# Eight long products, then eight short ones: the order of matmuls within a projection's chunk

## Chip, cores and metric

The kernel runs on one core of one Trainium2 chip. The metric is the device time of one execution in microseconds, from the start of the program to its end.

## What is computed

Two layers of an encoder on 256 tokens with 1024 channels, in float32. Cut to what matters here:

```python
def layer(h):
    xn = rmsnorm(h, norm1)                       # 256 x 1024
    u, q, k, v, g_pool, g_attn = split(xn @ w_in)  # 1024 -> 1024 + 3*1536 + 2*1024
    pool_out = (windowed_means(u) - u) @ w_pool * pool_scale
    attn_out = dilated_attention(q, k, v, rel_bias)       # 12 heads in 3 groups
    merged = sigmoid(g_pool) * (pool_out @ w_a) + sigmoid(g_attn) * (attn_out @ w_b)
    h = h + merged @ w_o
    a, g = split(rmsnorm(h, norm2) @ w_up)       # 1024 -> 2 * 2816
    return h + (gelu(conv3(a)) * g) @ w_down     # 2816 -> 1024
```

A last rmsnorm follows the second layer. The weights are some 162 MB in all and are read once.

## The kernel before

All large products use a faster float32 format of TensorE that keeps fewer bits (`F32R`). To keep the accuracy, each operand is written as a high part and a rest, `a = ah + al` and `w = wh + wl`, and a product is made of three: `wh*ah + wh*al + wl*ah`.

The class `Weights` brings the weights. SyncE loads pieces of 1 MB into one of three `raw` buffers. ScalarE casts half of such a piece into `wh` (L177), and VectorE subtracts to make `wl` (L178). There are five buffers each of `wh` and `wl`, and the splits run some three pieces ahead of TensorE. A buffer is free again when the last matmul that reads it has run.

A *chunk* is 128 output channels of a projection, for all 256 tokens. `proj` takes the next piece, of shape 128 x 8 x 128 (`KD` = 8 steps of 128 input channels), and calls `two_sums`. The normalised input lies in `x2`, channels on partitions, as [128, 8, part, 256 tokens], so that the high parts and the rests of one step stand side by side as 512 columns. `two_sums` makes, for each of the eight steps, one matmul with `wh` on all 512 columns (L482), which writes `wh*ah` into the left half and `wh*al` into the right half of one PSUM tile, and one matmul with `wl` on the 256 columns of high parts (L483), which adds `wl*ah` to the right half. All 16 add up in the same tile, `proj_ps`. Then ScalarE copies the right half out (L503) and VectorE adds the left (L504), or like steps in the attention's query and key code. There are four such PSUM tiles.

`proj` is called 192 times: for the pooled branch's input, the queries and keys, the projection with `w_a` (input `po`), both gates and both halves of `w_up`. The product with `w_b` (`b_ps`, input `at`) calls `two_sums` too, 16 times, with four steps instead of eight. Other products do not go through it: the values (L578, L653, L740) and the residual products with `w_o` and `w_down` (L508 to L510) have runs of 512 columns, and the pooled product (L474 to L476) and the attention have 256 columns or 128.

The attention's work is cut into steps (`scores`, `turn`, `weigh`) which are called between chunks. `turn` transposes the probabilities on TensorE (L903), eight of 128 columns for a head.

Each engine runs its own queue in order. A scheduler of the tile framework sets the order within each queue as the program is built, by an estimate of when operands will be there; on TensorE it may put other matmuls between those of one chunk.

Of the kernel before, what the change touches and what calls it, by code (L numbers as in the profile page):

```python
# [204 lines left out]
def encoder(ctx, tc, x, w_in, w_pool, pool_scale, w_a, w_b, w_o, norm1, norm2, w_up, conv_w,  # L205
# [272 lines left out]
    def two_sums(ps, wh, wl, x2, nk):  # L478


        for k in range(nk):
            nc.tensor.matmul(ps, wh(k), x2[:, k], start=(k == 0), stop=False)  # L482
            nc.tensor.matmul(ps[:, 1], wl(k), x2[:, k, 0], start=False, stop=(k == nk - 1))  # L483

    def proj(x2):

        i, (wh, wl) = W.get()
        ps = mmp.tile([P, 2, S], F32, tag="mm", name="proj_ps")
        two_sums(ps, lambda k: wh[:, k, :], lambda k: wl[:, k, :], x2, KD)
        W.free(i)  # L490
        return ps[:, 0], ps[:, 1]
# [256 lines left out]
    for l in range(DEPTH):  # L748
# [251 lines left out]
        for c4 in range(2):  # L1000
            ths = [gate(4 * c4 + j) for j in range(4)]
            for j2 in range(2):
                i, (wh, wl) = W.get()
                for j in range(2):
                    c = 4 * c4 + 2 * j2 + j
                    ps = mmp.tile([P, 2, S], F32, tag="mm", name="b_ps")
                    cc = slice(j * P, (j + 1) * P)
                    two_sums(ps, lambda k: wh[:, k, cc], lambda k: wl[:, k, cc], at2, 4)
                    m = sm.tile([P, S], F32, tag="u", name="m")
                    add_up(m, (ps[:, 0], ps[:, 1]))  # L1010
                    nc.vector.scalar_tensor_tensor(
                        out=m, in0=ths[2 * j2 + j], scalar=1.0, in1=m, op0=ALU.add, op1=ALU.mult
                    )
                    nc.vector.tensor_add(out=m, in0=m, in1=pa[:, c, :])
                    m = halves(m)
                    nc.scalar.copy(out=mh[:, c], in_=m)
                    nc.vector.tensor_sub(out=ml[:, c], in0=m, in1=mh[:, c].bitcast(F32))
                W.free(i)
# [152 lines left out]
```

## Time and profile before

| | us |
|---|---|
| median of 3 runs | 885.79 (885.66 to 886.0) |
| the profiled execution | 885.33 |
| its span | 883.5 |
| TensorE busy (PE) | 875.9, 99% of the span |
| weight loads (PEld) | 755.9, 86% |
| VectorE busy (DVE) | 676.8, 77% |
| ScalarE busy (ACT) | 520.2, 59% |
| DMA | 164.47 MB, 186 GB/s |
| granted clock of TensorE | 0.998 |

PE is TensorE's matmuls, and PEld its weight loads, which run beside them. A row of a group names the line, the engine and operation, the tiles (out<-in), the shapes and the count, then the busy time and the mean duration in ns, then the idle time before it. The line numbers are those of the kernel before. Starts in the timeline are in us from the start of the span; in the trace they are whole nanoseconds, and where single steps are given in ns they are differences of two such starts. Matmuls are pipelined and overlap, so that the step from one start to the next is shorter than the duration.

Where the stages lie, in us of the span: first values until 41, pooled input 41 to 79, queries, keys, attention and the projection with `w_a` 79 to 178, gates and `w_b` 179 to 234, `w_o` 234 to 257, the MLP 257 to 442; the second layer in the same order from 442 on, with its MLP from 691 to 877.

### The profile page before, as it was taken

What the parts mean: (1) busy time and instruction counts of PE and PEld (TensorE: products, weight loads), DVE (VectorE), ACT (ScalarE), POOL (GpSimd) and SP (SyncE); (2) the same over time, 40 slices, a digit from 0 to 9 for tenths busy, and PEclk for the clock granted to TensorE, in tenths of its full rate; (3) what the DMA queues carried; (4) which work ended last, traced back from release to release, by engine and by line L of the source; (5) the groups of instructions that cost most, each with busy time, mean ns of one, the idle gap of its engine ahead of it and who ended that gap; (6) DMA issues with size and microseconds to landing.
All of it is one profiled execution on the core that took longest, in us unless ns stands there. A gap on an engine that the chain in (4) does not pass through costs nothing.

```text
span 883.5 us, 12773 instructions
## 1 busy us (share of the span) xinstructions
PE 875.9 (99%) x4849; PEld 755.9 (86%) x4849; DVE 676.8 (77%) x1151; ACT 520.2 (59%) x913; POOL 13.1 (1%) x40
## 2 busy tenths in 40 slices
PE   9999999999999999999999999999999999999997
PEld 7889889888888888888888898889888888888886
DVE  6988785767869977877855977766778698787784
ACT  7745554556647756666645564554566477666663
POOL 1000000000000000000000000000000000000000
PEclk9999999999999999999999999999999999999999
DMA  9669744455555475465736555444556447455541
GB/s 332 230 205 307 239 145 144 143 179 188 185 187 191 146 236 190 154 227 191 239 119 213 168 191 191 143 152 134 191 191 218 156 154 231 172 198 187 187 144 48
DMA packets 125790, 164.47 MB, mean 186 GB/s; under 512 B 2995, under 2 KB 106107, under 8 KB 125600
## 3 DMA queue, kind: packets, MB, share of 16 engines
q1 hardware_dynamic: 125712, 163.65, 55.7%
q8 instruction: 38, 0.62, 0.3%
q14 instruction: 24, 0.20, 0.1%
q10 hardware_dynamic: 16, 0.00, 0.0%
HBM read 162.57 MB, written 3.69 MB: 188 GB/s over the span
## 4 chain that ended last, share of the span: by engine, by line
PE 99%; ACT 0%; POOL 0%; DVE 0%; issue 0%; POOLq 0%; ACTq 0%
PE proj_ps L482 41%; PE proj_ps L483 20%; PE res_ps L508 6%; PE res_ps L510 6%; PE v_ps L578 6%; PE res_ps L509 6%; PE v_ps L740 2%; PE b_ps L482 2%; PE v_ps L653 1%; PE pt_ps L903 1%; PE b_ps L483 1%; PE o_ps L924 1%; PE s_ps L874 1%; PE s_ps L869 1%; PE o_ps L920 1%; PE xt_ps L450 1%
## 5 line engine op out<-in xcount | busy, mean ns | idle before, releaser
L482 PE MATMUL proj_ps<-x,wh 128*128 128x512 f32 x1408 | 498.5, 398 | 0.0
L178 DVE TENSOR_TENSOR wl<-raw,wh 128x1024 fp32r<-128x1024 f32 x274 | 334.4, 1223 | 123.5 <-ACT wh L177 121.3
L177 ACT CAST wh<-raw 128x1024 fp32r<-128x1024 f32 x274 | 286.6, 1051 | 189.4 <-PE proj_ps L482 146.2
L483 PE MATMUL proj_ps<-x,wl 128*128 128x256 f32 x1408 | 394.1, 280 | 0.0
L482 PEld LDWEIGHTS proj_ps<-x,wh 128*128 128x128 f32 x1408 | 264.5, 188 | 63.6 <-issue 0.7
L483 PEld LDWEIGHTS proj_ps<-x,wl 128*128 128x128 f32 x1408 | 265.6, 189 | 0.9 <-issue 0.2
L508 PE MATMUL res_ps<-wh,actq 128*128 128x512 f32 (+1 forms) x184 | 70.5, 383 | 0.0
L510 PE MATMUL res_ps<-wh,actk 128*128 128x512 f32 (+1 forms) x184 | 70.1, 381 | 0.0
L509 PE MATMUL res_ps<-wl,actq 128*128 128x512 f32 (+1 forms) x184 | 70.0, 380 | 0.0
L482 PE MATMUL proj_ps<-po,wh 128*128 128x512 f32 x128 | 46.2, 402 | 0.0
L510 PEld LDWEIGHTS res_ps<-wh,actk 128*128 128x128 f32 x184 | 34.6, 188 | 7.0
L508 PEld LDWEIGHTS res_ps<-wh,actq 128*128 128x128 f32 x184 | 34.6, 188 | 6.9
L509 PEld LDWEIGHTS res_ps<-wl,actq 128*128 128x128 f32 x184 | 34.6, 188 | 6.2
L483 PE MATMUL proj_ps<-po,wl 128*128 128x256 f32 x128 | 35.7, 279 | 0.0
L1084 ACT ACTIVATE y<-a,prm 128x256 f32<-128x256 f32 x36 | 21.6, 599 | 18.9 <-DVE a L504 18.8
L1101 ACT ACTIVATE y<-y 128x256 f32<-128x256 f32 x44 | 18.3, 416 | 21.3 <-DVE y L1098 21.3
L482 PEld LDWEIGHTS proj_ps<-po,wh 128*128 128x128 f32 x128 | 24.0, 188 | 5.0
L416 ACT ACTIVATE junk<-h 128x512 f32<-128x512 f32 (+1 forms) x20 | 10.9, 547 | 27.7 <-DVE h L414 27.7
L508 PE MATMUL res_ps<-wh,m 128*128 128x512 f32 (+1 forms) x72 | 26.5, 368 | 0.0
L510 PE MATMUL res_ps<-wh,m 128*128 128x512 f32 (+1 forms) x72 | 26.3, 366 | 0.0
L509 PE MATMUL res_ps<-wl,m 128*128 128x512 f32 (+1 forms) x72 | 26.3, 365 | 0.0
L578 PE MATMUL v_ps<-wh,x 128*128 128x512 f32 x80 | 25.7, 392 | 0.0
(208 smaller groups left out, 1129.6 us busy)
## 6 DMA issues: line engine op xcount, KB each, us to landing
raw<-in_w_in_dram SPq DMA_DIRECT2D x58, 1024.0 KB, 5.4
raw<-in_w_up_dram SPq DMA_DIRECT2D x44, 1024.0 KB, 5.1
raw<-in_w_down_dram SPq DMA_DIRECT2D x22, 1024.0 KB, 4.9
raw<-in_w_a_dram SPq DMA_DIRECT2D x8, 1024.0 KB, 4.9
raw<-in_w_o_dram SPq DMA_DIRECT2D x8, 1024.0 KB, 4.9
raw<-in_w_b_dram SPq DMA_DIRECT2D x4, 1024.0 KB
sk<-fd SPq DMA_DIRECT2D x1, 2560.0 KB
raw<-in_w_pool_dram SPq DMA_DIRECT2D x2, 1024.0 KB
```

What stands on the lines that cost most here:

```text
L177: lambda: nc.scalar.copy(out=h, in_=src),
L178: lambda: nc.vector.tensor_sub(out=l, in0=src, in1=h.bitcast(F32)),
L416: nc.scalar.activation(junk[:, 0 : cc.stop - cc.start], h[:, t, cc], AF.Square, scale=D**-0.5, accum_out=ss[:, n : n + 1],)
L482: nc.tensor.matmul(ps, wh(k), x2[:, k], start=(k == 0), stop=False)
L483: nc.tensor.matmul(ps[:, 1], wl(k), x2[:, k, 0], start=False, stop=(k == nk - 1))
L508: nc.tensor.matmul(ps, ah, wh, start=first, stop=False)
L509: nc.tensor.matmul(ps, ah, wl, start=False, stop=False)
L510: nc.tensor.matmul(ps, al, wh, start=False, stop=last)
L578: nc.tensor.matmul(ps, x2[:, 2 * n + j, part, t, :], w[:, j, :], start=(n + m == 0), stop=(n == 3 and m == 5),)
L740: nc.tensor.matmul(ps[t], a[:, k, t, :], w[:, j, :], start=(k + m == 0), stop=(k == KD - 1 and m == 2),)
L1084: nc.scalar.activation(y, a, AF.Identity, bias=b, scale=w1)
L1101: nc.scalar.activation(y2, y2, AF.Tanh, scale=c)
```

## The change

In `two_sums` the loop over the steps is split into two. The eight products with `wh` on 512 columns come first, and then the eight with `wl` on 256 columns. In `b_ps` it is four and four. What is added up is the same; the order of the additions in the right half of the tile differs.

```diff
     def two_sums(ps, wh, wl, x2, nk):
 
 
         for k in range(nk):
             nc.tensor.matmul(ps, wh(k), x2[:, k], start=(k == 0), stop=False)
+        for k in range(nk):
             nc.tensor.matmul(ps[:, 1], wl(k), x2[:, k, 0], start=False, stop=(k == nk - 1))
```

## Prediction

> **What bounds the kernel now.** I read the page's totals first, then the chain, the groups and the waits.
>
> ```profile
> span 883.5 us, 12773 instructions
> PE 875.9 (99%) x4849; PEld 755.9 (86%) x4849; DVE 676.8 (77%) x1151; ACT 520.2 (59%) x913; POOL 13.1 (1%) x40
> PE 99%; ACT 0%; POOL 0%; DVE 0%; issue 0%; POOLq 0%; ACTq 0%
> L482 PE MATMUL proj_ps<-x,wh 128*128 128x512 f32 x1408 | 498.5, 398 | 0.0
> L177 ACT CAST wh<-raw 128x1024 fp32r<-128x1024 f32 x274 | 286.6, 1051 | 189.4 <-PE proj_ps L482 146.2
> L483 PE MATMUL proj_ps<-x,wl 128*128 128x256 f32 x1408 | 394.1, 280 | 0.0
> ```
>
> TensorE is the bound from the first microsecond to the last six. Idle time before the two product groups is 0.0. All its waits together are two:
>
> ```profile
> PE gain_ps L333 <- DVE ones L319: 1.0, 1, 1.0
> PE v_ps L653 <- ACT xuh L609: 0.2, 1, 0.2
> ```
>
> So time can only come from, or go to, the spacing of matmuls. The durations of the groups (398 and 280 ns) do not give it, since matmuls overlap; the step from one start to the next in the timeline does. In two stretches where nothing but pairs of a 512 and a 256 column product runs, with the clock at full speed in both:
>
> ```profile
> 181.58 0.39 PE L482 MATMUL proj_ps<-x,wh 128*128 128x512 f32 x1
> ...
> 209.31 0.39 PE L482 MATMUL proj_ps<-x,wh 128*128 128x512 f32 x1
> ```
>
> ```profile
> 286.80 0.40 PE L482 MATMUL proj_ps<-x,wh 128*128 128x512 f32 x1
> ...
> 300.93 0.40 PE L482 MATMUL proj_ps<-x,wh 128*128 128x512 f32 x1
> ```
>
> The first holds 10 chunks of 8 pairs: 27.73 us / 80 = 346.6 ns a pair. The second holds 5 chunks: 14.13 us / 40 = 353.3 ns. The instructions are the same; the layout of the start times is not. In the tight rhythm the steps are 231 and 112 ns, then 233 and 117, and so on; in the loose one 233 and 117, 241 and 120, 236 and 113, repeated. A pair costs 6.7 ns more there.
>
> What would runs of one width cost? The down projection (L508 to L510) gives runs of 512 columns, the pooled product (L474 to L476) a run of 256:
>
> ```profile
> 387.67 0.40 PE L508 MATMUL res_ps<-wh,actq 128*128 128x512 f32 x1
> ...
> 390.00 0.39 PE L509 MATMUL res_ps<-wl,actq 128*128 128x512 f32 x1
> ...
> 391.36 0.39 PE L509 MATMUL res_ps<-wl,actq 128*128 128x512 f32 x1
> ```
>
> ```profile
> 512.10 0.28 PE L475 MATMUL pool_ps<-pll,wh 128*128 128x256 f32 x1
> ...
> 513.06 0.40 PE L482 MATMUL proj_ps<-x,wh 128*128 128x512 f32 x1
> 513.29 0.28 PE L483 MATMUL proj_ps<-x,wl 128*128 128x256 f32 x1
> ```
>
> From 390.00 on, six steps take 1.36 us: 226.7 ns each, and it stays there. But the first ten, right behind the pairs, take 2.33 us: 233.1 each (241, 237, 234, 236, 224, 231, 236, 228, 233, 231). A run of 512 therefore begins with a settling time of up to 64 ns. The run of 256 is at 0.96 us / 8 = 120.0 ns, and the 512 behind it takes 233. 226.7 + 120.0 = 346.7 is exactly the tight pair. I call that the base, and all above it the excess.
>
> **The change, part by part.** Nothing is added or removed: 4849 matmuls and loads before and after, each with its own load. In the built program the chunks stand on TensorE in the same order, except that one chunk in each layer's attention, which was cut in two by transposes, is now whole.
>
> *Excess now.* I took every step of the 1597 pairs, less 226.7 or 120.0. 43 steps are more than 40 ns over (the first product behind 128 column transposes, 313 ns instead of 227, and the bias products); they are 3.6 us and stay. The rest is 6.46 us: 0.55 in 79 to 112 us, 1.99 in 269 to 441, 1.16 in 479 to 545, 1.99 in 703 to 876, 0.78 in the attention and early stretches, and nothing in 59 to 79, 179 to 234 and 612 to 668, which are in the tight rhythm. This is all that a new order can win.
>
> *Excess after.* A chunk becomes eight steps of 512 behind a run of 256, then eight of 256 behind a run of 512. The second join is in the trace at 874 us and twice more: 113, 119, then 120 throughout, 8 ns below the base. The first step of the first join is too: 233 ns, 7 over. How a run of 512 goes on from there is not, since the trace has only a 256 next. Bounds: from above, the ten steps at 387.67, whose first eight are 54 ns over; from below, the entry at 303.76, 236 and then at once 227, 9 ns over. Between them lies the entry of 234.27 (231, 224, 231, 236, 228, 232, 231, then 227), 27 ns over. I line the unknown run up with places where a 512 starts in the same phase. Settled starts keep one place on a grid of 6.67 ns (the tight pair is 52 such units, the loose one 53), and the start behind the 233 lies up to a nanosecond short of the settled place; in the trace, starts there go on 236, 228, 232, 231, 227 more often than straight to 227. So I take 7 + 20 = 27 over, less the 8 of the short run: 20 ns a chunk, three units, between 0 and 46.
>
> - 192 chunks of `proj` x 20 ns = 3.84 us.
> - 16 half chunks of `b_ps`, now at the base: 7 + 9 + 2 + 5 in four steps, less 8: 15 ns, +0.24 us.
> - 16 runs of the down projection now follow a run of 256 and not pairs: 14 settle in 27 instead of 64 ns, two in 27 instead of 9: -0.48 us.
> - The two whole chunks save one return from transposes each, 86 ns: -0.2 us with what goes with it.
> - Removed: 6.46 us.
>
> The sum is 3.84 + 0.24 - 0.48 - 0.2 - 6.46 = -3.06 us. Against the profiled execution's 885.33 (883.5 of span and 1.8 around it) that is 882.3; the median of the runs is 0.46 higher, so 882.7.
>
> [...]
>
> *Costed at nothing.* ScalarE splits a weight (L177) when its `wh` buffer is free, which comes 7 x 120 = 0.84 us earlier; 146.2 us of its idle time wait for that, but TensorE never waited for the splits, so this is only more lead; the loads on SyncE follow the split and keep their order. `wl` is needed 7 x 227 = 1.6 us later than before, so VectorE's L178 gets lead too. The last product of a chunk is still a 256 into the second half, so the reads (L503, L504) start as before. VectorE's and ScalarE's own orders shift around the attention. The one tight place:
>
> ```profile
> 119.73 0.48 DVE L891 TENSOR_SCALAR p<-p,rz 128x512 f32<-128x512 f32 x1
> 120.28 0.64 PE L903 MATMUL pt_ps<-ident,p 128*128 128x128 f32 x4
> ```
>
> The second four transposes start 0.07 us behind their input. They now stand right behind the first four, 0.7 us earlier, and the cut chunk no longer covers them. In the new order of VectorE the scaling L891 stands one weight split (1.22 us) earlier, which covers it. Without that cover it costs 0.7 us a layer, 1.4 in all, everything behind it on TensorE included.
>
> **The rivals.**
>
> *No settling time.* Behind the 233 the run goes straight to 227, as at 303.76. Each chunk is then at the base: -6.46 - 0.8 (down projection) - 0.2 = -7.5, 878.3 us. For it: the start lies less than a nanosecond from the settled place. Against: most starts there go on unsettled.
>
> *Every chunk settles anew, at length.* As at 387.67: each of the eight steps of 512 pays about a unit, and the short run behind it undoes the settling, so that the next chunk pays again. 192 x (54 - 8) = 8.83, b_ps 16 x (41 - 8) = 0.53, less 6.46 and 0.2: +2.7, 888.5 us. For it: 14 of 16 entries behind pairs go this way, and the eight steps end before the ten of settling do. Against: those entries start with 241, not 233. It decides from 34 ns a chunk on (6.46 us / 192), five units. The stretches that are now in the tight rhythm would lose, 2.77 to 2.82 us a chunk.
>
> *Order is free.* The excess has a cause outside the order (who starts when, which rhythm a stretch fell into), and the mean of tight and loose stays: 885.8, or a few tenths beside it. Four or five units a chunk give much the same. [...] For it: three stretches of pairs are at the base already. Against: the rhythm changes where the widths change, behind runs.
>
> **How the numbers follow.** Forecast 0.42, no settling 0.14, order free or near the break-even 0.17, settling at length 0.27. The likeliest gives 882.7; its own range is two to four units, 881.4 to 884.0 at 1.28 us a unit (192 x 6.67 ns). The range that leaves out 2 in 10 takes in both outer cases: 878.2 to 888.6. About 0.2% (1.8 us) is what a measurement of this kernel can tell from no change. Faster: 0.14 and most of 0.42, 0.52. Same: 0.17 and the slow edge of the forecast, 0.20. Slower: 0.28.
>
> **What would show it.** Step by step: chunks at 2.79 us from start to start everywhere, in the stretches of 179 to 234 us (2.773 now) as in 269 to 441 (2.826 now); inside a chunk 233, 236, 228, 232, 231, 227, 227, 227 and 113, 119, 120. The first stretch should get slower by 0.3 us and the second faster by 1.2. Chunks all at 2.773 show the first rival, at 2.82 the second, unlike chunks in unlike stretches the third. An idle TensorE before L903 or L482 would be the lost cover. I am wrong if the step behind a long run of 256 is not 226.7 to 241 ns at all, for example if eight short products in a row outrun their weight loads and go above 120.

## The result, and the profile after

| | before | changed |
|---|---|---|
| median of 6 runs, us | 885.71 (885.02 to 886.0) | 881.88 (881.74 to 882.35) |
| the profiled execution, us | 885.33 | 882.29 |
| its span, us | 883.5 | 880.5 |

The ratio of the medians is 0.996, with a 95% interval of 0.995 to 0.997. The changed kernel is faster by 3.8 us by the medians and by 3.0 us between the two profiled executions. The forecast was 882.7 us, and 882.3 for a profiled execution.

The page of the changed kernel, its totals, chain and groups:

```profile
span 880.5 us, 12819 instructions
PE 872.5 (99%) x4849; PEld 759.1 (86%) x4849; DVE 676.9 (77%) x1151; ACT 520.3 (59%) x913; POOL 13.8 (2%) x40
PE 99%; ACT 0%; POOL 0%; DVE 0%; issue 0%; POOLq 0%; ACTq 0%
...
L482 PE MATMUL proj_ps<-x,wh 128*128 128x512 f32 x1408 | 354.1, 393 | 0.0
...
L484 PE MATMUL proj_ps<-x,wl 128*128 128x256 f32 x1408 | 196.3, 282 | 0.0
```

TensorE still carries 99% of the chain, and the two product groups still have no idle time before them. What looks like a large change is none: the busy time of L482 fell from 498.5 to 354.1 us and that of the short products from 394.1 to 196.3 us, though the mean of one instruction hardly moved (398 to 393 ns, 280 to 282 ns). Overlapping records of one line are now neighbours, and busy time counts an overlap once. All of PE fell by only 3.4 us, which is the real gain.

The waits of TensorE are the same two:

```profile
PE gain_ps L333 <- DVE ones L319: 1.0, 1, 1.0
PE v_ps L654 <- ACT xuh L610: 0.2, 1, 0.2
```

So the time came out of the spacing of matmuls. The timeline of TensorE in the two stretches that the prediction showed (start, time, instruction):

```profile
181.54 2.00 PE L482 MATMUL proj_ps<-x,wh 128*128 128x512 f32 x8
...
209.47 0.86 PE L482 MATMUL proj_ps<-x,wh 128*128 128x512 f32 x3
```

```profile
284.21 2.00 PE L482 MATMUL proj_ps<-x,wh 128*128 128x512 f32 x8
286.05 1.12 PE L484 MATMUL proj_ps<-x,wl 128*128 128x256 f32 x8
...
300.97 0.86 PE L482 MATMUL proj_ps<-x,wh 128*128 128x512 f32 x3
```

From 181.54 to 209.47 are ten chunks in 27.93 us, 2.793 each (2.773 before): this stretch became slower. From 284.21 to 300.97 are six chunks in 16.76 us, also 2.793 each (2.826 before). Unlike stretches have become alike. Inside a chunk the eight long products take 1.84 us and the eight short ones 0.95. By single starts the steps are 233, 236, 228, 233, 231, 226, 227, 227 and then 113, 119, 120 six times: 20 ns above the base. Of the 191 chunks whose products stand in one piece, 143 take 2793 or 2794 ns from their first start to the next product's.

Eighteen chunks are cheaper. Seventeen stand behind a run of 512, as this one behind the values (L579); the other is the kernel's first, with only two small transposes between:

```profile
269.82 1.98 PE L482 MATMUL proj_ps<-x,wh 128*128 128x512 f32 x8
271.63 1.12 PE L484 MATMUL proj_ps<-x,wl 128*128 128x256 f32 x8
272.59 0.60 PE L1059 MATMUL a_turn<-ident,a_rows 128*128 128x128 f32 x4
```

From 269.82 to 272.59 is 2.77 us: the width does not change at the chunk's start, all eight long steps are 226 or 227, and the short run begins with 113 as everywhere.

### The profile page after: what moved, and what is told of

Its sections match the earlier page's. It is cut to its first block, busy times and chain, and to the rows that moved or that the text cites. A ratio compares the mean times of both kernels' runs of the same rounds, so it can differ in the third digit from the quotient of the medians.

```text
span 880.5 us, 12819 instructions
## 1 busy us (share of the span) xinstructions
PE 872.5 (99%) x4849; PEld 759.1 (86%) x4849; DVE 676.9 (77%) x1151; ACT 520.3 (59%) x913; POOL 13.8 (2%) x40
## 4 chain that ended last, share of the span: by engine, by line
PE 99%; ACT 0%; POOL 0%; DVE 0%; issue 0%; POOLq 0%; ACTq 0%
PE proj_ps L482 40%; PE proj_ps L484 21%; PE res_ps L510 6%; PE res_ps L509 6%; PE v_ps L579 6%; PE res_ps L511 6%; PE v_ps L741 2%; PE b_ps L482 2%; PE v_ps L654 1%; PE b_ps L484 1%; PE s_ps L875 1%; PE o_ps L925 1%; PE pt_ps L904 1%; PE s_ps L870 1%; PE o_ps L921 1%; PE xt_ps L450 1%
## 5 line engine op out<-in xcount | busy, mean ns | idle before, releaser
L482 PE MATMUL proj_ps<-x,wh 128*128 128x512 f32 x1408 | 354.1, 393 | 0.0
L482 PEld LDWEIGHTS proj_ps<-x,wh 128*128 128x128 f32 x1408 | 254.1, 189 | 47.4 <-issue 0.5
L484 PEld LDWEIGHTS proj_ps<-x,wl 128*128 128x128 f32 x1408 | 192.0, 190 | 13.8
L484 PE MATMUL proj_ps<-x,wl 128*128 128x256 f32 x1408 | 196.3, 282 | 0.0
L482 PE MATMUL proj_ps<-po,wh 128*128 128x512 f32 x128 | 33.1, 400 | 0.0
L482 PEld LDWEIGHTS proj_ps<-po,wh 128*128 128x128 f32 x128 | 22.9, 189 | 4.1
L579 PE MATMUL v_ps<-wh,x 128*128 128x512 f32 x80 | 25.7, 392 | 0.0
L1086 DVE SCALAR_TENSOR_TENSOR y<-a,prm,y 128x255 f32<-128x255 f32 x36 | 17.2, 479 | 8.1 <-ACT y L1085 8.1
```

The lines of the kernel that those rows point to most:

```text
L579: nc.tensor.matmul(ps, x2[:, 2 * n + j, part, t, :], w[:, j, :], start=(n + m == 0), stop=(n == 3 and m == 5),)
L1086: nc.vector.scalar_tensor_tensor(out=y[:, 1:], in0=a[:, : S - 1], scalar=w0, in1=y[:, 1:], op0=ALU.mult, op1=ALU.add)
```

## Experiments

The theory is the prediction's: a change of width costs TensorE a *settling* of some steps, short ones give some of it back, and what a chunk costs above the base depends on how its widths are laid out. The rivals are three: the gain is the lead that the splits of the weights got (`wl` needed later, `wh` free earlier); the excess belongs to alternating two weights rather than two widths; or it belongs to stretches and not to the order.

For each kernel I added up the excess of all steps behind products of `proj` (a start to the next, less 226.7 or 120.0; steps over 40 ns left out, as in the prediction). It is 6.42 us before and 3.34 in the changed kernel. (The prediction has 6.46 for the first; a base of 226.67 ns in place of 226.7 makes about that difference.) The *stream* is the time from the first product of the first chunk to the start of the last matmul, in the profiled execution of each kernel. It leaves out the start of the program, which no order here touches and which took 41.6 to 42.4 us in these executions. The kernel before, run again beside each, gave medians of 885.2 to 885.6 us.

| kernel | us, median | stream, us | proj excess, us | chunk in the MLP behind short products, ns above its base |
|---|---|---|---|---|
| before: runs of 1 | 885.7 | 835.0 | 6.42 | 37 to 58 |
| runs of 2 | 880.15 | 829.9 | 2.29 | 13 |
| runs of 4 | 884.64 | 833.8 | 5.24 | 33 |
| changed: runs of 8 | 881.88 | 831.3 | 3.34 | 20 |
| one long first | 884.17 | 833.1 | 3.93 | 20 |
| two chunks: runs of 16 | 881.79 | 831.2 | 1.53 | 10 |
| two chunks outside | 880.59 | 830.0 | 2.08 | 10 |
| steered | 879.79 | 829.2 | 0.85 | 0 in most, 5 to 8 in others |

**The lead or the layout.** One long product, then the eight short ones, then the other seven long. The runs have the changed kernel's lengths, read cyclically, but `wl` is needed as early as before.

```diff
-        for k in range(nk):
-            nc.tensor.matmul(ps, wh(k), x2[:, k], start=(k == 0), stop=False)
+        nc.tensor.matmul(ps, wh(0), x2[:, 0], start=True, stop=False)
         for k in range(nk):
-            nc.tensor.matmul(ps[:, 1], wl(k), x2[:, k, 0], start=False, stop=(k == nk - 1))
+            nc.tensor.matmul(ps[:, 1], wl(k), x2[:, k, 0], start=False, stop=False)
+        for k in range(1, nk):
+            nc.tensor.matmul(ps, wh(k), x2[:, k], start=False, stop=(k == nk - 1))
```

> Each chunk is one 512, eight 256, seven 512. Across chunks that is again one run of eight 512 (seven of one chunk, one of the next) and one run of eight 256, as in the changed kernel, but wl is needed after one product instead of eight and wh comes free at the end. Settling theory (the cost is paid once per join of a short run to a long one, whatever the place of the join in the chunk): again 2.793 us from chunk to chunk, total within 0.5 us of the changed kernel, 881.4 to 882.4 us. Lead theory (the gain came from wh coming free early and wl being wanted late): the gain goes back, 885 to 886 us, with idle time of TensorE before the first 256 of a chunk.

Measured: 884.17 us (883.82 to 885.36), 0.9989 of before, 0.998 to 0.9998. The total lies between the ranges of both theories, so neither had it; the spacing decides. In the timeline of this kernel:

```profile
276.17 0.39 PE L481 MATMUL proj_ps<-x,wh 128*128 128x512 f32 x1
276.39 1.11 PE L483 MATMUL proj_ps<-x,wl 128*128 128x256 f32 x8
...
298.51 0.39 PE L481 MATMUL proj_ps<-x,wh 128*128 128x512 f32 x1
```

Eight chunks from 276.17 to 298.51 are 22.34 us, 2.793 each, the changed kernel's chunk without its lead, and the waits view has no wait ahead of a short product. So the lead is not the gain. But the stream of matmuls is 1.8 us longer than the changed kernel's, elsewhere. The largest piece, 0.74 us, is a wait of transposes at the end of the first layer's MLP. In the waits view and in VectorE's timeline:

```profile
PE xt_ps L450 <- DVE xn L441: 0.5, 1, 0.5
```

```profile
440.46 0.48 DVE L441 SCALAR_TENSOR_TENSOR xn<-h,rstd,gain 128x256 f32<-128x256 f32 x1 [1.85 <-POOL rstd L428]
440.87 0.68 DVE L414 TENSOR_TENSOR h<-res_ps,h 128x512 f32<-128x512 f32 x1
441.47 1.27 DVE L441 SCALAR_TENSOR_TENSOR xn<-h,rstd,gain 128x256 f32<-128x256 f32 x3
```

The scheduler put the sum L414 in front of three of the four normalisations; in the changed kernel three normalisations come first:

```profile
439.14 1.28 DVE L441 SCALAR_TENSOR_TENSOR xn<-h,rstd,gain 128x256 f32<-128x256 f32 x3 [1.84 <-POOL rstd L428]
440.34 0.68 DVE L414 TENSOR_TENSOR h<-res_ps,h 128x512 f32<-128x512 f32 x1
```

Another 0.57 us are the transposes of the probabilities, which wait behind VectorE too, and 0.59 the proj steps. These places are read from the profile; no kernel tested them by themselves. An order in `two_sums` also reorders VectorE; the two waits here are 1.3 us, a third of the 3.7 us by which the changed kernel's stream is shorter than that of before.

**Shorter runs.** In groups of four and four; the kernel of twos has 2 for each 4 of the new lines:

```diff
-        for k in range(nk):
-            nc.tensor.matmul(ps, wh(k), x2[:, k], start=(k == 0), stop=False)
-        for k in range(nk):
-            nc.tensor.matmul(ps[:, 1], wl(k), x2[:, k, 0], start=False, stop=(k == nk - 1))
+        for k0 in range(0, nk, 4):
+            for k in range(k0, k0 + 4):
+                nc.tensor.matmul(ps, wh(k), x2[:, k], start=(k == 0), stop=False)
+            for k in range(k0, k0 + 4):
+                nc.tensor.matmul(ps[:, 1], wl(k), x2[:, k, 0], start=False, stop=(k == nk - 1))
```

> Four 512, four 256, four 512, four 256 in a chunk: twice the joins. Settling theory: the 4 + 4 products of b_ps in the changed kernel cost 16.6 ns over the base, so a chunk costs 2 x 16.6 = 33 ns over it instead of 20: 2.806 us a chunk, 192 x 13 ns = 2.5 us more than the changed kernel, 884.4 us. Order-is-free theory: no difference to the changed kernel, 881.9, or the old time, 885.7.

> Two 512 and two 256 in turn: four joins a chunk. Settling theory: the first two steps of a settling run are 7 and 9 ns over, and the two of the short run some 4 to 8 under: 8 to 12 ns a join, 32 to 48 a chunk against 20 now and some 34 on the average in turn: 2.805 to 2.821 us a chunk, 884.2 to 887.3 us. Order-is-free theory: 881.9 or 885.7, with different chunks in different stretches.

Fours: 884.64 us (884.26 to 885.44), as expected. A chunk has the steps 233, 236, 228, 233 | 117, 119, 118, 117 | 235, 233, 236, 224 | 117, 120, 120, 120, or 33 ns over the base.

Twos: 880.15 us (880.04 to 880.78), a miss by 4 us, and on the good side. In the timeline four groups of two and two make a chunk:

```profile
283.97 0.63 PE L483 MATMUL proj_ps<-x,wh 128*128 128x512 f32 x2
284.44 0.39 PE L485 MATMUL proj_ps<-x,wl 128*128 128x256 f32 x2
...
286.75 0.63 PE L483 MATMUL proj_ps<-x,wh 128*128 128x512 f32 x2
```

From 283.97 to 286.75 is 2.78 us (2786 or 2787 ns by starts). The steps are 233, 236 | 116, 112 | 233, 231 | 113, 119. Two long steps are 16 or 11 ns over the base, and the two short ones behind them give back 12 or 8; I had expected them to give back 4 to 8. So a price for each change of width does not hold: twos have four times as many changes as the changed kernel and cost less. What a change costs hangs on where the settling is cut off and on the place at which the next run starts.

**Width or weights.** In turn again, but with `wl` on all 512 columns too: one more term is added (`wl*al`, and `wl*ah` now goes to the left half), and the widths are all the same.

```diff
         for k in range(nk):
             nc.tensor.matmul(ps, wh(k), x2[:, k], start=(k == 0), stop=False)
-        for k in range(nk):
-            nc.tensor.matmul(ps[:, 1], wl(k), x2[:, k, 0], start=False, stop=(k == nk - 1))
+            nc.tensor.matmul(ps, wl(k), x2[:, k], start=False, stop=(k == nk - 1))
```

> In turn as before, but the product with wl takes all 512 columns (it adds the term wl*al to the left half of the reading order's second half too, so the kernel does one term more than it needs). All products of the stream are then of one width, while wh and wl still alternate. Width theory: no excess, every step 226.7 ns, a chunk 16 x 226.7 = 3.627 us flat, total 881.9 + 192 x 0.834 + 16 x 0.42 = 1049 us. Theory that the alternating weights or the alternating PSUM regions make the excess: steps stay above 226.7 by some 3 ns on the average, as in the loose pairs, a chunk 3.66 to 3.68 us, total 1055 to 1059 us.

Measured: 1050.01 us in one run. In the timeline the weights alternate and the starts are even:

```profile
339.80 0.39 PE L482 MATMUL proj_ps<-x,wh 128*128 128x512 f32 x1
340.02 0.39 PE L483 MATMUL proj_ps<-x,wl 128*128 128x512 f32 x1
...
347.96 0.39 PE L482 MATMUL proj_ps<-x,wh 128*128 128x512 f32 x1
```

36 steps in 8.16 us are 226.7 ns each. What excess is left (0.98 us in all) stands in chunks that follow something else than a run of 512: 0.21 us behind the pooled run of 256, and 0.76 behind the attention's products and transposes. The other way round, 24 products of 256 columns a chunk, `wh` loaded twice:

```diff
         for k in range(nk):
-            nc.tensor.matmul(ps, wh(k), x2[:, k], start=(k == 0), stop=False)
-        for k in range(nk):
+            nc.tensor.matmul(ps[:, 0], wh(k), x2[:, k, 0], start=(k == 0), stop=False)
+            nc.tensor.matmul(ps[:, 1], wh(k), x2[:, k, 1], start=False, stop=False)
             nc.tensor.matmul(ps[:, 1], wl(k), x2[:, k, 0], start=False, stop=(k == nk - 1))
```

> In turn, but every product 256 columns wide: the 512 is cut into its two halves, so a chunk has 24 products and wh is loaded twice. Width theory: no excess, every step 120.0 ns, a chunk 24 x 120 = 2.880 us flat in all stretches, total 881.9 + 192 x 0.087 + 16 x 0.037 = 899.2 us. Theory that the alternating weights or PSUM halves make the excess: a loose rhythm again, some stretches 50 ns a chunk above others, 903 to 909 us.

Measured: 901.47 us in one run, 2.3 us over the expectation. The steps are what the theory said, 120.0 ns throughout and 2880 ns a chunk; in the timeline 26 steps take 3.12 us:

```profile
289.77 0.28 PE L484 MATMUL proj_ps<-x,wl 128*128 128x256 f32 x1
289.89 0.28 PE L482 MATMUL proj_ps<-x,wh 128*128 128x256 f32 x1
...
292.89 0.28 PE L483 MATMUL proj_ps<-x,wh 128*128 128x256 f32 x1
```

The stream of matmuls is 17.8 us longer than the changed kernel's; the rest of the surplus is outside it or in the scatter of a single run, and I leave it there. Both kernels say the same: within one width there is no loose rhythm, and two weights in turn cost nothing.

**Longer runs.** Two chunks at a time, 16 long products into two tiles and then 16 short ones:

```diff
+    second = []
     def proj(x2):
-        i, (wh, wl) = W.get()
-        ps = mmp.tile([P, 2, S], F32, tag="mm", name="proj_ps")
-        two_sums(ps, lambda k: wh[:, k, :], lambda k: wl[:, k, :], x2, KD)
...
+        if second:
+            return second.pop()
+        got = [W.get() for _ in range(2)]
+        tiles = [mmp.tile([P, 2, S], F32, tag="mm", name="proj_ps") for _ in range(2)]
+        for ps, (i, (wh, wl)) in zip(tiles, got):
+            for k in range(KD):
+                nc.tensor.matmul(ps, wh[:, k, :], x2[:, k], start=(k == 0), stop=False)
+        for ps, (i, (wh, wl)) in zip(tiles, got):
+            for k in range(KD):
+                nc.tensor.matmul(ps[:, 1], wl[:, k, :], x2[:, k, 0], start=False, stop=(k == KD - 1))
...
+        second.append((tiles[1][:, 0], tiles[1][:, 1]))
+        return tiles[0][:, 0], tiles[0][:, 1]
```

> Two chunks at a time: sixteen 512 (eight into each of two tiles), then sixteen 256. Half as many joins. Settling theory: 27 ns of settling less 8 once per two chunks instead of once per chunk, so a pair of chunks takes 5.567 us instead of 5.587, and 96 x 20 ns = 1.9 us come off the changed kernel: 880.0 us. Lead theory (buffers and lookahead count): two weight pieces are held at once and only three are ahead, so TensorE begins to wait for the splits: 882 us or more, with waits before L-lines of the products.

Measured: 881.79 us (881.1 to 882.48), a miss: no better than the changed kernel. The excess fell as worked out, 3.34 to 1.53 us. But the waits view has two new lines:

```profile
PE pool_ps L474 <- DVE q L983: 0.9, 1, 0.9
PE proj_ps L496 <- DVE po L861: 0.5, 1, 0.5
```

Both stand in the first layer, at 88.31 and 89.84 us, in the stage of the queries and keys where the pooled product is made. The pooled product's steps are 1.89 us over the base (0.00 in the changed kernel), with the wait ahead of the chunk behind it counted in: the gain went into waits behind VectorE. In the code `pool_ps` and `proj_ps` share four PSUM tiles, and two chunks at a time hold two of them; that this is the reason was not tested by itself. If the waits belong to that stage, two chunks at a time everywhere but in the queries, keys and `w_a` should keep the rest (`proj(x2, 1)` in those two calls):

> Two chunks at a time as in the run before, but not in the stage of the queries, keys and pooled product and not with w_a, where single chunks stay, as in the changed kernel. In the run before, the settling fell by 1.8 us as worked out and 1.9 us came back as waits of TensorE, two of them (1.1 and 0.7 us) in the pooled product at 87 and 89 us and one (0.5 us) at the first chunk with w_a. Theory that these waits come from holding two chunks in that stage: they are gone, 64 of the 96 halved joins are kept, 64 x 20 ns = 1.3 us under the changed kernel, 880.6 us. Theory that two chunks at a time cost elsewhere too (late reads of the sums, fewer splits ahead): 881.9 us or more, with waits in other places.

The wait of 0.5 us is in fact ahead of a chunk with `x` (L496 at 89.84 us), not of one with `w_a`.

Measured: 880.59 us (880.13 to 880.78), as expected. The excess is 2.08 us, and of the waits one of 0.2 us is left at the pooled product, whose steps are 0.47 us over the base. Against the changed kernel the medians differ by 1.3 us, but as ratios to the kernel before, run beside each, the two are 0.9947 (0.9934 to 0.9961) and 0.996 (0.995 to 0.997), which overlap; the stream, 1.3 us shorter, is the better evidence.

**Choose the rhythm.** If the loose rhythm of before is a matter of how a stretch of pairs is entered, a few groups of four and four in front of it should set it right. This kernel takes the products in turn as before. Behind a run of 256 its first four steps are a group of four and four; behind a run of 512 the first two such; behind the transposes at the entry of the MLP three. `behind` is set to 1, 2 or 3 at these places, and to 0 behind the attention's transposes.

```diff
+    behind = [0]
     def two_sums(ps, wh, wl, x2, nk):
-        for k in range(nk):
-            nc.tensor.matmul(ps, wh(k), x2[:, k], start=(k == 0), stop=False)
-        for k in range(nk):
-            nc.tensor.matmul(ps[:, 1], wl(k), x2[:, k, 0], start=False, stop=(k == nk - 1))
+        fours = min(behind[0], nk // 4)
+        behind[0] -= fours
+        runs = [4] * fours + [1] * (nk - 4 * fours)
+        k0 = 0
+        for n in runs:
+            for k in range(k0, k0 + n):
+                nc.tensor.matmul(ps, wh(k), x2[:, k], start=(k == 0), stop=False)
+            for k in range(k0, k0 + n):
+                nc.tensor.matmul(ps[:, 1], wl(k), x2[:, k, 0], start=False, stop=(k == nk - 1))
+            k0 += n
```

> Pairs in turn as in the kernel before, but behind a run of other products the first steps are made in fours: one group of 4 + 4 behind a run of 256 (the pooled product), two behind a run of 512 (down projection, values), three behind the transposes of the MLP's entry. In the kernel with runs of four, such groups lead to a step of 235 ns, and in the kernel before, a pair that begins with 235 goes on in the tight rhythm (230 and 117) each of the five times. Settling theory: the stretches of pairs that were loose become tight, 2.773 us a chunk between 90 and 112, 280 and 303 us and within the MLP's groups of four, instead of 2.826; of the excess of 6.47 us some 1.2 is left, and the down projection's settling halves: 879.9 us, at least 1 us under the changed kernel. Theory that the rhythm belongs to the stretch (its buffers, its other engines' work): those stretches stay at 2.826, 884 to 886 us.

Measured: 879.79 us (879.37 to 880.38), 0.9934 of before, 0.9921 to 0.9946. In the timeline, the last group and the stretch of pairs behind it:

```profile
275.64 0.63 PE L492 MATMUL proj_ps<-x,wl 128*128 128x256 f32 x4
276.11 0.40 PE L490 MATMUL proj_ps<-x,wh 128*128 128x512 f32 x1
...
302.46 0.39 PE L519 MATMUL res_ps<-wh,actq 128*128 128x512 f32 x1
```

From 276.11 to 302.46 are 76 pairs in 26.35 us, 346.7 ns a pair, where the kernel before took 353.3. The steps alternate between 230 and 117. Only the order of products inside a few chunks differs from before, and 5.6 us of excess are gone. This has the lowest median of all; it beats both kernels, and its advantage over the changed kernel is 2.1 us by the medians. The range of the twos (880.04 to 880.78) overlaps its own.

## Why the prediction was right

Its sign, its mechanism and the steps of a chunk held for runs of eight. A price for other lengths did not come with it: by the same settling the twos were put at 884.2 to 887.3 us, and they took 880.15. Where it lay beside the measurement, step by step, in us (the changed kernel's trace less that of before):

| step of the sum | forecast | measured |
|---|---|---|
| excess of the pairs removed, 192 chunks settle instead | 3.84 - 6.46 = -2.62 | 3.34 - 6.42 = -3.08 |
| `b_ps` | +0.24 | +0.27 |
| runs of the down projection | -0.48 | -0.46 |
| two returns from transposes fewer | -0.2 | -0.21, of which 0.16 come back in the next row |
| the transposes' own steps | 0 | -0.30 (0.46 of waits gone, 0.16 given back) |
| stream, with a small rest | -3.06 | -3.67 |
| ahead of the first chunk, and behind the last matmul | 0 | +0.27 and +0.36 |
| profiled execution | -3.06 | -3.04 |

*Excess after.* The forecast steps were 233, 236, 228, 232, 231, 227 and 113, 119, 120, and the trace has just these, within one nanosecond. Lining the unknown run up with places of equal phase gave the right one of the three layouts between 0 and 46 ns a chunk. The term was mis-sized because I let all 192 chunks settle. Eighteen begin settled (17 behind a run of 512, and the first) and are 27 ns cheaper: 18 x 27 = 0.49 us, and 3.84 less that is 3.35.

*b_ps.* A chunk of four and four is 0.27 us / 16 = 17 ns over, 15 forecast.

*The down projection.* Behind the short run, its steps are 233, 236, 228, 233, 230, 227: 27 ns, and each of the 16 runs begins so.

*Returns from transposes, and their cover.* Here the price was wrong, though the sum came out close. I took a return at 86 ns, from the first product's 314 ns instead of 227. The step before it, from the last transpose's start to that product's start, is 28 or 29 ns instead of 109, in all eight returns of the changed trace and all ten of before. The two together are 342 ns against 336: a return costs 6 ns, and two fewer save nothing that counts. What did save time is the transposes' input. The timeline of TensorE at the place that the prediction called tight:

```profile
119.24 1.03 PE L904 MATMUL pt_ps<-ident,p 128*128 128x128 f32 x8
120.03 1.18 PE L482 MATMUL proj_ps<-x,wh 128*128 128x512 f32 x4
```

The eight stand in one run, at 108 or 109 ns from start to start, so the cover held: L892 (L891 of before) ends at 119.29, 0.4 us ahead of the fifth transpose. Before, the step of the fifth transpose or the one ahead of it was long at four places (151 ns at 120.3 us, 261 and 138 at 158.4, and 157, 266 and 137 in the second layer), 0.46 us in all above 109 a step. These are gone. It was luck: the order and timing on VectorE fell out well, and the prediction had looked at one of the places only for a loss. In the first experiment the same places fall out worse (398 and 393 ns).

*The ends.* I had costed the start and the tail at nothing. They took back 0.63 us, about as much as the pairs and the transposes had gained beyond the forecast. No chunk stands ahead of the first 42 us, so the 0.27 there is not the new order's work as far as the traces show (that stage took 41.6 to 42.4 us over ten kernels, one execution each); the cause of the 0.36 stays open. That the profiled execution came out to 0.01 us is therefore luck in part; the saving in the stream, which is what the change touches, was underestimated by 0.6 us. The medians differ by 3.83, and the remaining 0.8 us lie within the scatter of single executions (885.02 to 886.0, 881.74 to 882.35).

*The rivals.* No settling: only the 18 chunks that begin settled look like it. Every chunk settles at length: no, the start at 233 goes the short way everywhere. Order is free: no, the same products in eight orders gave 879.8 to 885.7 us, so a gap that hangs on a product's own width alone does not hold where widths are mixed. Within one width, once settled, the gap is fixed here, 226.7 and 120.0 ns. The Trainium skill (TensorE: Matmul & The Clock Gate, section "Back-to-back issue gap") gives N / 2.4 + 2.5 ns for an isolated warm matmul of N columns. An estimate from it is 215.8 and 109.2 ns, and the steps measured here are 11 ns above both.

## What to carry to other kernels

Where TensorE is the bound and products of two widths alternate, read the steps from start to start, not the busy time: the same instructions can sit in a tight or a loose rhythm for a whole stretch (28 us of the one and 14 of the other were shown above), and the few products at the entry can decide which. The least invasive cure is to steer the entry of a stretch (here a few groups of four and four), and the next is to make runs of one width; neither gain is proportional to the number of changes, so try several lengths. Compare the waits view after any such reordering, since the order of products also moves the other engines' queues: with one long product first, waits took 1.3 us, and with two chunks at a time the whole of the further gain.

## What the runs showed of the hardware

*Starts lie on a grid.* In settled runs of 512 columns of the kernel before, the starts of the whole execution taken modulo 20/3 ns (6.67) fall together: their mean resultant length, which is 1 for equal phases and near 0 for random ones, is 0.89 over 850 us, and 0.14 with a period of 6.666 ns instead. The tight pair is 52 of these units and the loose one 53, and over a whole chunk settling costs whole units: 20 ns are three, the 33 of the fours five and the 13 of the twos two. The runs counted lie among other widths and transposes, so starts keep the grid through these. What it is in hardware stays open; no experiment here tells that.

*A constant on each product.* 226.7 and 120.0 ns for 512 and 256 columns are 106.7 apart, 0.417 ns a column. If the time grows evenly with the columns, which two widths cannot show, 13.3 ns (two units) remain with each product. The transposes of the probabilities, 128 columns of float32, step at 109 ns (108 to 110).

*Returning from transposes is nearly free.* Behind the transposes of the probabilities the first product of 512 columns takes 312 to 316 ns in the changed kernel, but starts 28 or 29 ns behind the last transpose instead of 109. A step read alone shows a loss of 87 ns; the two steps together show 6.

*Short products in a row do not outrun their loads.* In the kernel with products of 256 only, weight loads are busy 94% of the span and the steps still stay at 120.0 ns over whole stretches, so they do not go above it, as the end of the prediction feared. Whether the loads have a part in the 120.0 itself is not shown.
